# Two-layer hybrid decoder trunk: the second MLP product in pairs of half steps, its block sums on GpSimd, and the joint softmax issued earlier

## The chip, the cores and the metric

The kernel runs on one core of one Trainium2 chip. The metric is device time in microseconds (us) of one execution; the median of several is given, and one profiled execution is looked into. Engines: TensorE (PE), VectorE (DVE), ScalarE (ACT), GpSimd (POOL), and SyncE (SP), which issues most DMAs.

## What is computed

Two layers over 1024 tokens of width 1024, all in float32. The reference, cut to its core:

```python
for i in range(2):
    hn = rmsnorm(h, norm1[i])
    z = hn @ w_in[i]                       # u (256) | q, k, v (768 each)
    q, k = partial_rotary(q), partial_rotary(k)
    pool_out = pool_mixer(u, pool_w[i], pool_scale[i])   # windows 2, 4, 8, 16
    attn_out = dilated_mixer(q, k, v)      # 3 head groups, softmax over the groups' lse
    h = h + concat([pool_out, attn_out]) @ w_out[i]
    hn = rmsnorm(h, norm2[i])
    h = h + square(relu(hn @ w_up[i])) @ w_down[i]       # 1024 -> 4096 -> 1024
    gate = sigmoid(rmsnorm(h, norm3[i]) @ w_gate[i])
    h = h + gate * (p[i] @ w_ple[i])
return rmsnorm(h, final_norm)
```

In `dilated_mixer` three head groups (window 128, 512, 2048 at dilation 1, 4, 16) each give an output and a log-sum-exp; a softmax over the three log-sum-exps weighs the outputs.

## The kernel before, in words

Activations lie transposed, as tiles of 128 features by 1024 tokens. A float32 value is split into a high part (fp32r) and the rest, and a product is three matmuls (high x high, high x low, low x high) of 128x128 weights and 128x512 tokens. `split` makes the parts of an activation: ACT copies the high part, DVE subtracts (L500 to L506).

**One layer** on TensorE: the in-projection with the attention of three groups between (`attend`), the last value columns (`v2p`, L976 to L981), the out-projection (`po`), the up product (banks X, Y, Z with operand `xP`), the down product (banks X, Y, Z with operand `wP`), then gate and per-layer embedding (`gt`).

**Order.** One thread of Python issues everything. `Clock` holds a planned time: each matmul advances it (`tick`), generators (`ck.go`) issue other engines' operations and say with `yield ns` how long until their next one. `need` runs waiting generators until an operand has been issued. So the delays in nanoseconds set the order in which each engine gets its instructions; at run time the engines wait for each other by semaphores, and each engine keeps its order.

**Joint softmax** (`joint`, L897 to L928). After the 16 score statistics of each group, DVE takes the maximum over groups (L905, L906), subtracts (L908), ACT takes exp (L910), DVE sums and divides (L913 to L919), TensorE transposes the weights (`jt`, L922), DVE copies them out (`jw`, L925), a DMA writes them to DRAM (`wt_d`). `spread` reads them back, broadcast over 64 partitions (`wb`, from `W_0` on), `weigh` multiplies the head outputs (L950) and splits them for the out-projection.

**Both MLP products** use seven products in place of eight for blocks two by two (`Seven`, `products7`). `Seven.sums` forms four sums of weight blocks on POOL (L280 to L287), `make` splits each of the seven weight operands (ACT L299, DVE L301). A product `P1` to `P7` of a set goes to bank X, or to Y (`P2`) or Z (`P7`, `P4`); `Set.open` takes the bank, and `close` evacuates it after every product, because the next product into the same bank accumulates onto it. Tags: X has 3 banks ("mm"), Y and Z two each ("s", "e").

**Up product**: 16 sets of 256 features, each 7 products of 4 blocks x 3 matmuls. Its operands `xP` are made by `combine` and `xpiece` from the residual (L1007, L1009, L1071 to L1079). `Up.close` copies or adds banks into `y1` and `y2` (ACT L1131, DVE L1139 to L1146); `relu` takes relu times the norm factor on DVE (L1154) and the square on ACT (L1157); `sums` forms four block sums on DVE (L1172 to L1178) and writes seven pieces to DRAM (`x_d`).

**Down product**: `x_back` reads a piece from `x_d`, ACT copies its high part (L1192), DVE subtracts (L1194), giving `wP`. `STEPS` lists steps (t, a, b): output rows 2t and 2t+1, blocks a to b. There are 19 a layer: (3,0,3), (2,0,2), (1,0,1), then (a mod 4, a, min(a+4, 16)) for a = 0 to 15. The products of a step follow one another, and `Down.close` adds each into `acc` on DVE (L1210), 7 additions a step. After the last step of a row pair `rest` splits the result for the gate and feeds the third norm.

Small blocks of work such as 128x1024 tiles come from one pool of 49 blocks.

Of the kernel before, what the change touches and what calls it, by code (L numbers as in the profile page):

```python
# [9 lines left out]
F32 = mybir.dt.float32  # L10
# [27 lines left out]
T_M1, W_0, W_1 = 13000.0, 11000.0, 1800.0  # L38
# [3 lines left out]
STEPS = [(3, 0, 3), (2, 0, 2), (1, 0, 1)] + [(a % 4, a, min(a + 4, 16)) for a in range(16)]  # L42
# [72 lines left out]
def body(nc, tc, pools, A, out):  # L115
# [107 lines left out]
    class Seven:  # L223
# [10 lines left out]
        def __init__(self, sets, seq, name, lead=(12, 6, 4)):  # L234
# [3 lines left out]
            self.first = {}  # L238
            for q, (j, _) in enumerate(seq):
                self.first.setdefault(j, q)  # L240
            self.kicks = {}
            for j, q in self.first.items():
                self.kick(q - load, lambda j=j: self.load(j))
                self.kick(q - sums, lambda j=j: ck.go(self.sums(j)))
            for q, (j, P) in enumerate(seq):
                self.kick(q - make, lambda j=j, P=P: ck.go(self.make(j, P), (name, j, P)))

        def kick(self, q, fn):
            self.kicks.setdefault(q, []).append(fn)

        def lead(self, ns, step):

            for q in sorted(k for k in self.kicks if k < 0):
                for fn in self.kicks[q]:
                    ck.at(max(0.0, ns + q * step), fn)

        def at(self, q):
            for fn in self.kicks.get(q, ()):
                fn()

        def load(self, j):
            src, k0, n, c0 = self.sets[j]
            self.raw[j] = []
            for t in range(2):
                r = blk(f"{self.name}r{t}", F32, (128, n, 2, 128))
# [3 lines left out]
                self.raw[j].append(r)  # L269

# [3 lines left out]
        def sums(self, j):  # L274
            a11, a12, a21, a22 = (self.block(j, t, k) for t in range(2) for k in range(2))
            n = self.sets[j][2]
            s = [blk(f"{self.name}s0", F32, (128, 2, n, 128))]
# [6 lines left out]
            s.append(blk(f"{self.name}s1", F32, (128, 2, n, 128)))  # L284
# [23 lines left out]
    for L in range(DEPTH):  # L308
# [13 lines left out]
        for m in range(8):  # L322
            groups.append([(wo, 0, 8, 128 * m, 128, None)])
        sevens.append(([(wu, 0, 4, 256 * j) for j in range(FF // 256)],
                       [(wd, a, b - a, 256 * t) for t, a, b in STEPS]))
# [264 lines left out]
    def layer(L, hT, norm, tabs):  # L590
# [289 lines left out]

        for m in range(2):
# [13 lines left out]

        jd = small.tile([128, 3, 8, 4], F32, name="jd", tag="jd", bufs=1)

        def joint():
            while stats != [16, 16, 16]:
                yield 500.0  # L900
            yield 1500.0
            mx = small.tile([128, 8, 4], F32, name="jm", tag="jm", bufs=1)
            lf = small.tile([128, 3, 8, 4], F32, name="jl", tag="jl", bufs=1)
            dn = small.tile([128, 8, 4], F32, name="jn", tag="jn", bufs=1)
# [587 lines left out]
```

## Time and profile before

| | before |
|---|---|
| runs, us | 2370.68, 2370.72, 2378.85 |
| median, us | 2370.72 |
| profiled execution, us | 2371.51 |
| its span (first to last instruction), us | 2369.7 |
| mean granted TensorE clock | 0.987 |
| busy: TensorE / DVE / ACT / POOL | 97% / 72% / 43% / 30% |
| instructions in the span | 30964 |

How to read it: TensorE is the engine with the least idle time, so its pauses are what an order of work can change. The busy shares are means over stages; the views of waits, of single stretches and of time order below tell where TensorE pauses and what it waits for. "Granted clock" is the TensorE clock that was granted in a stretch, as a share of full speed. A wait is named as waiting line <- line that ended it.

### The profile page before, as it was taken

The page shows a single profiled execution, that of the slowest core. Times are in us where ns is not written, and L with a number is a line of the kernel's source. Part 1 is how long each engine was busy: PE and PEld are TensorE (multiplying, and loading weights), DVE is VectorE, ACT ScalarE, POOL GpSimd, SP SyncE. Part 2 cuts the span into 40 slices and gives each one's busy share as a digit, 9 for nine tenths or more (in the row PEclk, how much of TensorE's full clock was granted, in tenths as well). Part 3 has the DMA queues.
Part 4 walks back from the last instruction along what each step waited for, and adds up shares of the span by engine and source line. Part 5 has one row for each costly group of instructions (what it writes and reads, how often), then busy time and mean ns, then how long its engine had stood idle before and what let it go on. Part 6 is the DMA issues. An engine that isn't in the chain of part 4 may idle for free.

```text
span 2369.7 us, 30964 instructions
## 1 busy us (share of the span) xinstructions
PE 2299.1 (97%) x11088; PEld 1850.5 (78%) x11088; DVE 1711.4 (72%) x2888; ACT 1007.9 (43%) x2161; POOL 713.5 (30%) x562
## 2 busy tenths in 40 slices
PE   8999999999999999989999999999999989999898
PEld 6767778788887788877887767887888868888788
DVE  7555667787778888886565466677777798888845
ACT  5244533443335344444324344434433354443545
POOL 5111126323332433342221122253333233332422
PEclk9999999999999999999999999999999999999999
DMA  5011133255448555521120111333444485553214
GB/s 178 19 46 19 38 90 107 67 165 158 155 150 285 160 158 158 149 67 45 55 63 19 37 37 38 90 119 103 154 156 156 155 286 152 158 157 107 85 54 134
DMA packets 292401, 268.31 MB, mean 113 GB/s; under 512 B 12092, under 2 KB 223672, under 8 KB 292248
## 3 DMA queue, kind: packets, MB, share of 16 engines
q1 hardware_dynamic: 289656, 262.70, 36.5%
q0 software_dynamic: 2272, 3.61, 0.9%
q8 instruction: 87, 1.43, 0.2%
q14 instruction: 66, 0.54, 0.1%
q10 hardware_dynamic: 320, 0.03, 0.0%
HBM read 193.65 MB, written 72.58 MB: 112 GB/s over the span
## 4 chain that ended last, share of the span: by engine, by line
PE 46%; DVE 4%; ACT 1%; POOL 1%; DMA 1%; issue 1%; SPq 0%; DVEq 0%; ACTq 0%; POOLq 0%
PE X L535 13%; PE Z L535 7%; PE Y L535 3%; PE in L520 3%; PE in L518 3%; PE in L522 3%; PE gt L522 2%; PE gt L520 2%; PE gt L518 2%; PE s L752 1%; PE o L788 1%; DMA wP<-x_d 1%; PE e L774 1%; PE pl L520 1%; PE pl L522 1%
## 5 line engine op out<-in xcount | busy, mean ns | idle before, releaser
L535 PE MATMUL X<-wP,d1p 128*128 128x512 f32 x768 | 186.7, 393 | 15.0 <-DVE acc L1210 14.4
L535 PE MATMUL X<-wP,d0p 128*128 128x512 f32 x768 | 188.7, 396 | 12.8 <-DVE acc L1210 11.9
L535 PE MATMUL X<-xP,u0p 128*128 128x512 f32 x768 | 186.2, 394 | 3.9 <-ACT y L1131 3.9
L535 PE MATMUL X<-xP,u1p 128*128 128x512 f32 x768 | 185.8, 394 | 3.9 <-ACT y L1131 3.9
L1194 DVE TENSOR_TENSOR wP<-wP 128x512 fp32r<-128x512 f32 x224 | 183.4, 821 | 5.1 <-ACT wP L1192 5.1
L535 PEld LDWEIGHTS X<-wP,d1p 128*128 128x128 f32 x768 | 143.4, 188 | 51.0 <-ACT d1p L299 10.2
L535 PEld LDWEIGHTS X<-wP,d0p 128*128 128x128 f32 x768 | 144.6, 190 | 48.9 <-ACT d0p L299 9.1
L535 PEld LDWEIGHTS X<-xP,u0p 128*128 128x128 f32 x768 | 146.2, 191 | 35.3 <-ACT y L1131 4.7
L535 PEld LDWEIGHTS X<-xP,u1p 128*128 128x128 f32 x768 | 145.9, 190 | 35.2 <-ACT y L1131 4.8
L1157 ACT ACTIVATE y<-y 128x1024 f32<-128x1024 f32 x64 | 67.5, 1055 | 221.5 <-DVE y L1154 221.5
L1192 ACT ACTIVATE wP<-wP 128x512 fp32r<-128x512 f32 x224 | 137.9, 620 | 43.7 <-DMA wP<-x_d 43.3
L188 DVE SCALAR_TENSOR_TENSOR wl<-wr,gt,wh 128x128 fp32r<-128x128 f32 (+1 forms) x288 | 118.7, 443 | 38.5 <-ACT wh L194 38.2
L647 POOL TENSOR_TENSOR rot<-rot,s 128x512 f32<-128x512 f32 x48 | 61.5, 1284 | 277.2 <-DVE rot L645 216.2
L1210 DVE TENSOR_TENSOR acc<-acc,X 128x512 f32<-128x512 f32 x152 | 103.5, 682 | 33.7 <-PE X L535 29.9
L765 ACT ACTIVATE sm<-sm,nm 128x128 f32<-128x128 f32 (+1 forms) x192 | 84.5, 442 | 93.3 <-DVE nm L762 93.1
L194 ACT ACTIVATE wh<-wr,gt 128x128 fp32r<-128x128 f32 (+1 forms) x304 | 104.2, 396 | 0.8 <-DMA wr<-in_w_in_dram 0.7
L758 DVE CUSTOM_DVE_ANT_0 sm<-s,cst 128x128 f32<-128x128 f32 (+1 forms) x192 | 58.3, 346 | 52.0 <-PE s L752 52.0
L535 PE MATMUL Z<-xP,u1p 128*128 128x512 f32 x384 | 94.6, 394 | 0.3 <-DVE xP L1009 0.2
L535 PE MATMUL Z<-xP,u0p 128*128 128x512 f32 x384 | 94.4, 394 | 0.3 <-DVE xP L1009 0.2
L535 PE MATMUL Z<-wP,d0p 128*128 128x512 f32 x384 | 93.5, 390 | 0.0
L535 PE MATMUL Z<-wP,d1p 128*128 128x512 f32 x384 | 93.4, 389 | 0.0
L535 PEld LDWEIGHTS Z<-xP,u1p 128*128 128x128 f32 x384 | 72.9, 190 | 16.3 <-DVE xP L1009 0.5
(474 smaller groups left out, 5982.7 us busy)
## 6 DMA issues: line engine op xcount, KB each, us to landing
wP<-x_d SPq DMA_DIRECT2D x224, 256.0 KB, 2.8
x_d<-ys SPq DMA_DIRECT2D x64, 512.0 KB, 3.5
wr<-in_w_in_dram SPq DMA_DIRECT2D x40, 512.0 KB, 3.8
u0r<-in_w_up_dram SPq DMA_DIRECT2D x32, 512.0 KB, 5.3
x_d<-y SPq DMA_DIRECT2D x32, 512.0 KB, 2.8
u1r<-in_w_up_dram SPq DMA_DIRECT2D x32, 512.0 KB, 5.3
d0r<-in_w_down_dram SPq DMA_DIRECT2D x26, 512.0 KB, 5.2
d1r<-in_w_down_dram SPq DMA_DIRECT2D x26, 512.0 KB, 5.8
```

The source lines that it names most:

```text
L188: nc.vector.scalar_tensor_tensor(l[:, k], raw[:, k], gs[k], f(h[:, k]), op0=OP.mult, op1=OP.subtract)
L194: nc.scalar.activation(h[:, k], raw[:, k], AF.Copy, scale=gs[k])
L518: nc.tensor.matmul(p, wh, h[:, cols], start=first and i == 0, stop=False)
L520: nc.tensor.matmul(p, wh, l[:, cols], start=False, stop=False)
L522: nc.tensor.matmul(p, wl, h[:, cols], start=False, stop=last and i == n - 1)
L535: nc.tensor.matmul(p, w[:, a, i], x[:, b], start=first and i == 0 and a == b == 0, stop=i == n - 1 and a == 1, skip_group_check=not first)
L647: nc.gpsimd.tensor_tensor(a, a, tb["s"][:, hs(hf)], op=OP.mult)
L765: nc.scalar.activation(sm[:, i, hh], sm[:, i, hh], AF.Exp, bias=nm[:, j:j + 1], scale=0.125, accum_out=ml[g][:, n, 4 + h:5 + h])
L1157: nc.scalar.activation(y, y, AF.Square)
L1192: nc.scalar.activation(t[:, 0], f(t[:, 1]), AF.Copy)
L1194: nc.vector.tensor_tensor(t[:, 1], f(t[:, 1]), f(t[:, 0]), op=OP.subtract)
L1210: nc.vector.tensor_tensor(a, a, p, op=OP.add)
```

## The change

1. **Down product.** `STEPS` becomes 18 steps (t, a, n blocks): (2,0,2), (3,0,2), fourteen steps of 4 blocks in which output row pairs 0 and 1 take blocks 0 to 3, then 2 and 3 blocks 2 to 5, and so on by pairs, then (2,14,2), (3,14,2). The products of the first two steps alternate, and those of the last two. `Seven` plans its loads, sums and pieces in nanoseconds of product time (675 per block) in place of numbers of products, and steps of two blocks share a tile.
2. **Evacuation of the down product.** `P1` and `P6` (one addition each) are copied by ACT to a tile `out`, and POOL adds it to `acc`; the other five additions of a step stay on DVE.
3. **Block sums** of `y` go from DVE to POOL. The last two up sets alternate product by product.
4. **x_back** of sets 0 to 3 is issued with the last 14 products of the up product; inside the down product two sets are read back after each odd step.
5. **Joint softmax**: the generator starts before the u tiles are evacuated, and its delays (1500, 900, 400, 1200, 400 ns between its parts) become 900, 1800, 700, 3400, 500; `W_0` goes from 11000 to 6000; a wb tile is released when both halves used it.
6. **Up start**: in `combine` for the last row pair, 4500 in place of 900 before `P5`; the out-projection's last four banks are ("mm", "o", "e", "e") in place of ("s", "s", "e", "e"). `norm3.start` 7000 in place of 3000.

### The diff, cut to its core

```diff
-T_M1, W_0, W_1 = 13000.0, 11000.0, 1800.0
+T_M1, W_0, W_1 = 13000.0, 6000.0, 1800.0
...
-STEPS = [(3, 0, 3), (2, 0, 2), (1, 0, 1)] + [(a % 4, a, min(a + 4, 16)) for a in range(16)]
+ORDER = ("P1", "P7", "P6", "P2", "P5", "P4", "P3")
+STEPS = [(2, 0, 2), (3, 0, 2)] + [(2 * (i // 2 % 2) + i % 2, i // 2 * 2, 4) for i in range(14)]
+STEPS += [(2, 14, 2), (3, 14, 2)]
...
+                self.begin.append(t)
+                t += 675.0 * sets[j][2]
...
+        def kick(self, q, ahead, fn):
+            self.kicks.append((self.begin[q] - 2700.0 * ahead, fn))
...
+        def two(self, name, n, shape):
+
+            if n > 2:
+                return [lambda i=i: blk(f"{self.name}{name}{i}", F32, (128, *shape)) for i in range(2)]
+            b = []
+
+            def part(i):
+                if not b:
+                    b.append(blk(f"{self.name}{name}", F32, (128, 2, *shape)))
+                return b[0][:, i]
+            return [lambda i=i: part(i) for i in range(2)]
...
+        jd = small.tile([128, 3, 8, 4], F32, name="jd", tag="jd", bufs=1)
+
+        def joint():
+            while stats != [16, 16, 16]:
+                yield 500.0
+            yield 900.0
...
+        ck.go(joint(), "joint", 500.0)
+
         for m in range(2):
             def u_evac(p, hf, m=m):
...
-            if hf == 1:
+            used.append((g, p))
+            if used.count((g, p)) == 2:
                 del wbc[g, p]
...
-        ck.go(joint(), "joint", 500.0)
...
             ck.go(xpiece(i, "P6", T2))
-            yield 900.0
+            yield 900.0 if i < 3 else 4500.0
             ck.go(xpiece(i, "P5", T1))
...
-        seq = first + [(j, P) for j in range(2, n7) for P in ("P1", "P7", "P6", "P2", "P5", "P4", "P3")]
+        seq = first + [(j, P) for j in range(2, n7 - 2) for P in ORDER]
+        seq += [(j, P) for P in ORDER for j in (n7 - 2, n7 - 1)]
...
-        outs = [(bank(f"po{L}", ("s", "e")[k // 2]), wk(ws[k % 2], range(8)), hs(k // 2)) for k in range(4)]
+        outs = [(bank(f"po{L}", ("mm", "o", "e", "e")[k]), wk(ws[k % 2], range(8)), hs(k // 2)) for k in range(4)]
...
-                sub = nc.vector.tensor_tensor
+                sub = nc.gpsimd.tensor_tensor
...
                 sub(s[0][:, 0], b22, b12, op=OP.subtract)
+                yield 1400.0
...
-                    m = 2 * self.t + n
+                    m = 2 * STEPS[self.j][0] + n
                     a = acc[m][:, hs(hf)]
+                    if P in ("P1", "P6"):
+                        if P == "P1":
+                            self.out = blk("out")
+                        o = self.out[:, hs(n)]
+                        nc.scalar.activation(o, p, AF.Copy)
+                        ck.go(self.later(a, o))
+                        continue
                     nc.vector.tensor_tensor(a, a, p, op=OP.add)
...
+            def later(self, a, o):
+                yield 700.0
+                nc.gpsimd.tensor_tensor(a, a, o, op=OP.add)
...
-        seq2 = [(k, P) for k in range(len(STEPS)) for P in ORDER]
+        nst = len(STEPS)
+        seq2 = [(k, P) for P in ORDER for k in (0, 1)]
+        seq2 += [(k, P) for k in range(2, nst - 2) for P in ORDER]
+        seq2 += [(k, P) for P in ORDER for k in (nst - 2, nst - 1)]
...
-                D7.lead(7 * 12 * 225.0, 2700.0)
-                early = [(i, P) for P in ORDER for i in range(3)] + [(3, P) for P in ORDER]
-                for n, (i, P) in enumerate(early):
-                    ck.at(3200.0 + 1150.0 * n, lambda i=i, P=P: ck.go(x_back(i, P)))
+                D7.lead(8 * 12 * 225.0)
+            n = q - len(seq) + 15
+            if n > 0 and n % 2 == 0:
+                for i in range(4):
+                    ck.at((0.0, 1400.0, 15000.0, 17500.0)[i], lambda i=i, P=seq[q][1]: ck.go(x_back(i, P)))
...
-            run(D7, seq2, [q], live, lambda k: xw[STEPS[k][1]:STEPS[k][2]])
-            if k >= 3 and s.a + 4 < 16:
-                ck.go(x_back(s.a + 4, P))
+            run(D7, seq2, [q], live, lambda k: xw[a:a + n])
+            if n == 4 and t % 2 and a + 4 < 16:
+                ck.go(x_back(a + 4, P))
+                ck.at(9500.0, lambda i=a + 5, P=P: ck.go(x_back(i, P)))
...
-        norm3.start(3000.0)
+        norm3.start(7000.0)
```

### How it moves instructions

**TensorE at the joint softmax, layer 0** (`v2p` are products of the last value columns, `jt` the transpose of the joint weights, `o` an attention output). Before:

```order
1161 L976 MATMUL v2p_2897<-wh_2665,h_7H 128x256
1162 L977 MATMUL v2p_2897<-wh_2665,h_7L 128x256
1163 L978 MATMUL v2p_2897<-wl_2666,h_7H 128x256
1164 L922 MATMUL jt_2941<-cst,jt 96x128
1165 L976 MATMUL v2p_2943<-wh_2663,h_0H 128x256
1166 L977 MATMUL v2p_2943<-wh_2663,h_0L 128x256
```

With the change:

```order
1139 L998 MATMUL v2p_2908<-wh_2664,h_0H 128x256
1140 L999 MATMUL v2p_2908<-wh_2664,h_0L 128x256
1141 L1000 MATMUL v2p_2908<-wl_2665,h_0H 128x256
1142 L927 MATMUL jt_2912<-cst,jt 96x128
1143 L998 MATMUL v2p_2908<-wh_2664,h_1H 128x256
1144 L999 MATMUL v2p_2908<-wh_2664,h_1L 128x256
1145 L1000 MATMUL v2p_2908<-wl_2665,h_1H 128x256
1146 L808 MATMUL o_2917<-et_2559,v_0_2420 64x128 x4
```

`v2p_2897` before is `v2p_2908` now: the transpose stood behind all 24 products of this tile, and now behind its first three.

**ACT a little later in the same place** (L500, now L520, copies the high part of a weighted head; L981, now L1003, evacuates `v2p`; L800, now L820, evacuates `o`). Before:

```order
223 L800 ACTIVATE o_0_2422<-o_2989 128x128
224 L800 ACTIVATE o_0_2423<-o_2989 128x128
225 L981 ACTIVATE v_0_2420<-v2p_2979,r_a_429 128x256
226 L500 ACTIVATE cat_0H<-o_0_878 128x512 x2
227 L800 ACTIVATE o_0_2422<-o_3036 128x128
228 L800 ACTIVATE o_0_2423<-o_3036 128x128
```

With the change:

```order
223 L820 ACTIVATE o_0_2422<-o_2992 128x128
224 L820 ACTIVATE o_0_2423<-o_2992 128x128
225 L520 ACTIVATE cat_0H<-o_0_879 128x512
226 L520 ACTIVATE cat_0H<-o_0_878 128x512 x2
227 L1003 ACTIVATE v_0_2420<-v2p_2985,r_a_429 128x256
228 L520 ACTIVATE cat_0H<-o_0_879 128x512
```

Three copies of weighted heads, which depend on the joint weights, now stand ahead of the fourth evacuation of `v2p`; before they stood behind it.

**POOL at layer 0's down start** (`d0s` sums of weight blocks, `ys` block sums of y, `acc` additions to the down output). Before, the twelve operations that follow the last sums of up weights:

```order
179 L280 TENSOR_TENSOR d0s_6074<-d0r_6055,d0r_6057 128x384
180 L282 TENSOR_TENSOR d0s_6074<-d0r_6057 128x384
181 L285 TENSOR_TENSOR d0s_6115<-d0s_6074,d0r_6055 128x384
182 L287 TENSOR_TENSOR d0s_6115<-d0r_6055,d0s_6115 128x384
183 L280 TENSOR_TENSOR d0s_6267<-d0r_6182,d0r_6184 128x256
184 L282 TENSOR_TENSOR d0s_6267<-d0r_6184 128x256
185 L285 TENSOR_TENSOR d0s_6311<-d0s_6267,d0r_6182 128x256
186 L287 TENSOR_TENSOR d0s_6311<-d0r_6182,d0s_6311 128x256
187 L280 TENSOR_TENSOR d0s_6429<-d0r_6365,d0r_6367 128x128
188 L282 TENSOR_TENSOR d0s_6429<-d0r_6367 128x128
189 L285 TENSOR_TENSOR d0s_6464<-d0s_6429,d0r_6365 128x128
190 L287 TENSOR_TENSOR d0s_6464<-d0r_6365,d0s_6464 128x128
```

With the change, twelve operations from the last sums of the first two steps on:

```order
238 L307 TENSOR_TENSOR d0s<-d0r,d0s 128x256 x2
239 L1195 TENSOR_TENSOR ys_6280<-y_5986,y_5939 128x512
240 L1243 TENSOR_TENSOR acc_0_6265<-acc_0_6265,out 128x512
241 L1197 TENSOR_TENSOR ys_6280<-y_5939 128x512
242 L300 TENSOR_TENSOR d0s_6320<-d0r_6233,d0r_6235 128x512
243 L1243 TENSOR_TENSOR acc_0_6296<-acc_0_6296,out 128x512
244 L1195 TENSOR_TENSOR ys_6331<-y_6007,y_5962 128x512
245 L1199 TENSOR_TENSOR ys_6281<-y_5986,ys_6280 128x512
246 L302 TENSOR_TENSOR d0s_6320<-d0r_6235 128x512
247 L1197 TENSOR_TENSOR ys_6331<-y_5962 128x512
248 L1202 TENSOR_TENSOR ys_6281<-y_5986,ys_6281 128x512
249 L305 TENSOR_TENSOR d0s_6363<-d0s_6320,d0r_6233 128x512
```

The small sums of the steps of three, two and one block are gone; block sums of the last two up sets and additions to `acc` stand between the weight sums of the first full step.

## Rows read from the trace of the kernel before

**Rows 1.** The page of the profile: span, and busy time of each engine.

```profile
span 2369.7 us, 30964 instructions
...
PE 2299.1 (97%) x11088; PEld 1850.5 (78%) x11088; DVE 1711.4 (72%) x2888; ACT 1007.9 (43%) x2161; POOL 713.5 (30%) x562
```

**Rows 2.** TensorE's waits: line, awaited line, total us, times, longest us.

```profile
PE X L535 <- DVE acc L1210: 26.3, 19, 5.2
PE jt L922 <- DVE jt L919: 11.0, 2, 5.5
PE X L535 <- ACT y L1131: 7.8, 4, 3.1
```

**Rows 3.** TensorE by stretch: start:end, length, busy (matmuls), granted clock, DMA share, GB/s.

```profile
307.60:314.40 6.80, 5.82 (x29) 0.50 0.18 54
440.80:447.60 6.80, 6.13 (x15) 0.50 0.00 0
748.00:751.40 3.40, 3.40 (x10) 0.50 0.65 246
1058.60:1065.40 6.80, 4.61 (x10) 0.50 0.58 190
1471.60:1478.40 6.80, 5.04 (x26) 0.50 0.23 67
1604.70:1611.50 6.80, 5.66 (x13) 0.50 0.00 0
1906.00:1921.00 15.00, 9.83 (x43) 1.00 0.86 310
2225.90:2229.30 3.40, 3.13 (x7) 0.50 0.67 207
```

**Rows 4.** Steady down product: stretch, length, busy of PE, PEld, DVE, ACT, POOL, clock.

```profile
800.00:1000.00 200.00, 200.00 (x884) 165.60 (x883) 173.58 (x222) 85.31 (x148) 68.15 (x44) 1.00 0.52 149
```

**Rows 5.** Order of time at layer 0's joint softmax: start, us, engine, line, [idle before].

```profile
295.74 0.69 DVE L883 TENSOR_TENSOR u<-in,rs_a 128x512 f32<-128x512 f32 x1 [0.96 <-PE in L522]
...
297.01 2.70 DVE L178 TENSOR_TENSOR wl<-wr,wh 128x1024 fp32r<-128x1024 f32 x1
...
300.29 1.83 DVE L905 TENSOR_TENSOR jm<-mlp,mlp 128x32 f32<-128x32 f32 x1
...
296.52 2.11 POOL L830 TENSOR_TENSOR pa<-u 128x896 f32<-128x896 f32 x1 [28.00 <-DVE u L883]
...
300.24 1.83 POOL L830 TENSOR_TENSOR pb<-pa 128x768 f32<-128x768 f32 x1
...
308.58 0.45 PE L922 MATMUL jt<-cst,jt 128*96 128x128 f32 x1 [5.51 <-DVE jt L919]
```

**Rows 6.** Order of time, DVE, from the transposed weights to the first weighted head.

```profile
309.06 0.29 DVE L925 COPY jw<-jt 96x128 f32<-96x128 f32 x1 [0.54 <-PE jt L922]
316.78 1.29 DVE L950 TENSOR_TENSOR o<-o,wb 128x512 f32<-128x512 f32 x2 [7.43 <-DMA wb<-wt_d]
```

**Rows 7.** Order of time, ACT, at layer 0's up start.

```profile
438.25 1.15 ACT L1007 ACTIVATE xP<-t 128x512 fp32r<-128x512 f32 x2 [1.42 <-DVE t L1075]
440.30 0.63 ACT L1007 ACTIVATE xP<-t 128x512 fp32r<-128x512 f32 x1 [0.90 <-DVE t L1079]
440.83 1.07 ACT L1131 ACTIVATE y<-X 128x512 f32<-128x512 f32 x2
```

**Rows 8.** Order of time, TensorE, at the end of layer 0's down product.

```profile
1049.78 1.61 PE L535 MATMUL X<-wP,d0p 128*128 128x512 f32 x6 [0.85 <-DVE acc L1210]
...
1060.65 1.62 PE L535 MATMUL X<-wP,d0p 128*128 128x512 f32 x3 [5.19 <-DVE acc L1210]
```

**Rows 9.** Order of time, DVE, at layer 0's down start.

```profile
746.24 0.68 DVE L1194 TENSOR_TENSOR wP<-wP 128x512 fp32r<-128x512 f32 x1
746.84 0.67 DVE L1210 TENSOR_TENSOR acc<-acc,X 128x512 f32<-128x512 f32 x1
```

**Rows 10.** POOL's weight sums (L280), layer 0 up: ns min/median/max, first and last start.

```profile
L280 POOL TENSOR_TENSOR u0s<-u0r,u0r x16: 1288/1294/1737, 409.4 to 694.9; 128x512 f32<-128x512 f32 x16
```

More of the change, by code (lines that the diff above doesn't have):

```diff
@@ L276, in sums @@
             n = self.sets[j][2]
[L277 removed]
+            ss = self.two("s", n, (2, n, 128))
+            s = [ss[0]()]
             add = nc.gpsimd.tensor_tensor
@@ L879, in mixed @@
                 ck.waiting.discard((id(cat[m][0]), hf))
+        jd = small.tile([128, 3, 8, 4], F32, name="jd", tag="jd", bufs=1)
[3 more added lines that the diff above has]
+            yield 900.0
+            mx = small.tile([128, 8, 4], F32, name="jm", tag="jm", bufs=1)
+            lf = small.tile([128, 3, 8, 4], F32, name="jl", tag="jl", bufs=1)
+            dn = small.tile([128, 8, 4], F32, name="jn", tag="jn", bufs=1)
+            nc.vector.tensor_tensor(mx, mlp[0][:, :, 0:4], mlp[1][:, :, 0:4], op=OP.max)
+            nc.vector.tensor_tensor(mx, mx, mlp[2][:, :, 0:4], op=OP.max)
+            for g in range(3):
+                nc.vector.tensor_tensor(jd[:, g], mlp[g][:, :, 0:4], mx, op=OP.subtract)
+            yield 1800.0
+            nc.scalar.activation(jd, jd, AF.Exp, scale=0.125)
+            yield 700.0
+            for g in range(3):
+                nc.vector.tensor_tensor(lf[:, g], mlp[g][:, :, 4:8], jd[:, g], op=OP.mult)
+            nc.vector.tensor_tensor(dn, lf[:, 0], lf[:, 1], op=OP.add)
+            nc.vector.tensor_tensor(dn, dn, lf[:, 2], op=OP.add)
+            nc.vector.reciprocal(dn, dn)
+            jt = small.tile([128, 3, 4, 8], F32, name="jt", tag="jt", bufs=1)
+            for g in range(3):
+                nc.vector.tensor_tensor(jt[:, g].rearrange("p h t -> p t h"), jd[:, g], dn, op=OP.mult)
+            yield 3400.0
+            p = bank(f"jt{L}", "e")
+            nc.tensor.transpose(p[:96, :128], jt.rearrange("p g h t -> p (g h t)"), ident)
+            yield 500.0
+            w = small.tile([96, 128], F32, name="jw", tag="jw", bufs=1)
+            nc.vector.tensor_copy(w, p[:96, :128])
+            yield 300.0
+            nc.sync.dma_start(out=wt_d, in_=w)
+            yield 2200.0
+        ck.go(joint(), "joint", 500.0)
         for m in range(2):
@@ L893, in layer @@
         ck.go(mixed(1), delay=T_M1)
[L896 to L904, printed above, removed]
[L905 to L930 removed]
+        wbc, used = {}, []
         def spread(g, p):
```

91 lines of the change are left out of this document (31 added, 60 removed).

## The prediction, made before the changed kernel was run

> **What bounds the kernel now.** I read the table of engines first. TensorE is busy 2299.1 of 2369.7 us, 97% [rows 1]; the other engines are far below that. So some 70 us is all that a change of order can win, and work on VectorE (DVE), ScalarE (ACT) or GpSimd (POOL) costs only where TensorE waits for it. The number of matmuls stays: seven products, and the block counts of a layer's steps add up to 64 before (3+2+1, thirteen of 4, 3+2+1) and after (2+2, fourteen of 4, 2+2).
>
> Second, TensorE's waits, longest total first [rows 2]. Three lines are what the edits touch: 26.3 us for a product bank that DVE has still to add into `acc` (L1210), 11.0 us (twice 5.5) for the joint softmax, 7.8 us for a bank that ACT has still to copy at the start of the up product. Together 45.1 us.
>
> Third, the granted clock behind these waits [rows 3]. After four of layer 0's pauses TensorE runs at 0.50, the lower of its two levels (1.2 of 2.4 GHz): 6.8 us after the joint softmax, 6.8 at the up start, 3.4 at the down start, 6.8 at the down end; in layer 1 6.8, 6.8 and 3.4 at the joint, up start and down end. That is 5 times 6.8 and twice 3.4, 40.8 us, in which half the work was done, so 20.4 us are lost to it. It does not follow every pause: from 1906 to 1921, at the down start of layer 1, TensorE was busy only 9.83 of 15 us and the clock stayed at 1.00. The ceiling of the change is 45.1 + 20.4 = 65.5 us, over both layers.
>
> Fourth, a steady stretch of the down product [rows 4]: TensorE busy 200.00 of 200.00 us (884 matmuls, 0.226 us each), DVE 173.58, POOL 68.15. Nothing is to be won there, and something could be lost.
>
> **The measure.** The profiled execution took 2371.51 us, 1.8 more than its span and 0.8 more than the median of the three runs, 2370.72. Terms are taken from 2371.5, and 0.8 comes off at the end.
>
> **Joint softmax (two layers).** Before, DVE's chain stood behind a split of weights of 2.70 us (L178) and two more operations, and its first maximum took 1.83 us, because a POOL addition of 1.83 us had begun just before it [rows 5]. TensorE came to the transpose at 303.0 and began it at 308.58, after 5.51 us. Now the maxima and differences come ahead of the last `u` evacuation, in a gap of 0.96 us in which DVE waited for TensorE at 294.8; the rest still meets the POOL additions that this evacuation releases. Some seven two-input operations then pass between POOL operations of up to 2.11 us: I put the end at 302.3. TensorE comes 3.2 us earlier (25 matmuls), at 299.7, and waits 2.6. Saved 2.9 a layer. What is late next: ACT's queue. Three copies that need the weighted heads now stand ahead of the fourth evacuation of v. Before, the first weighting came 7.7 us after jw (309.06 to 316.78), 7.43 us of it a wait for the wb DMAs [rows 6]. jw now comes behind a weight split, at about 306, so the weighting at 313.7, the copies at 315 and v at 317; a TensorE at full clock would be there at 313.5. So the half clock that might be given back here is eaten by this wait. I take 2.5 a layer, 5. Ends: 0 (jw no earlier) and 11.0 + 6.8 = 17.8 (wait and clock both gone). The later wb loads of `W_0` and the counted release of wb move no other wait: 0, the copies are hidden as before.
>
> **Up start.** ACT made four xP copies before the two y copies that TensorE waited for: it began at 438.25, stood 0.90 us for DVE, and came to y at 440.83 [rows 7]. With 4500 instead of 900 the last two xP copies come after the y copies, so y can be copied 2.0 us earlier, at 438.8; xP5 and xP4 then come later and could be waited for themselves. The last out-projection banks lie elsewhere, so that the second product no longer waits for one of them; as it may wait for an xP instead, I cost that at 0. Taken: 2.0 a layer, 4. Ends: 0, and 7.8 + 6.8 (two windows at half clock) = 14.6.
>
> **Down start.** Of the 26.3 us, the ends of the down products have 0.85 + 5.19 a layer [rows 8], 12.1 in two; 14.2 are left for the starts. There the products of one step of 3, 2 or 1 blocks followed each other into one bank X, and DVE came to the addition late (746.84) because it had block sums and splits of 0.60 us each back to back [rows 9]. Now two steps of two blocks alternate, so that a bank rests for a product of 6 matmuls (1.4 us) between two of its own, the x pieces of sets 0 to 3 start up to 36 us ahead, the eight block sums of the last two sets and two additions of seven leave DVE. They go to POOL: 16 POOL operations of 128x512 fall in the 96 matmuls (21.7 us) after the first down product: 8 block sums, 4 sums of weights, 4 additions to `acc`. At 1.29 each [rows 10] that is 20.6 us. DVE has 26 operations with two SBUF inputs there; at 0.60, too much for the twelve of 256 columns, 15.6 us. If the two engines exclude each other, as at 300 us [rows 5], 36.2 us want into 21.7: 14.5 us over. Pieces of weights are made three steps of 2.7 us ahead in the planner, 8.1 us; that leaves 6.4. Between 0 and 6.4 I take 3.2 a layer, the middle, as the block sums of the last sets are not needed until the last steps. Saved 14.2 - 6.4 = 8. Ends: 14.2 + 1.7 (the window of 3.4 at half clock) gained, and with 14.5 a layer 29.0 - 14.2 = 14.8 lost.
>
> The Trainium skill speaks against this part. Its page "Perfetto Trace Analysis", section "Optimizing Scalar/DVE Operations", says that moving operations between GpSimd and DVE might not help, since they share an SBUF read port. The trace agrees as far as rows 5 go: a maximum of 32 columns took 1.83 us. By that rule this term would be its lower end, and the time the second rival's; the additions from PSUM (L1210) would keep their pace.
>
> **Down end.** TensorE stood 0.85 and 5.19 us and then ran 6.8 us at half clock [rows 8, 3]: products of 9, 6 and 3 matmuls were shorter than what DVE had to do for each. Now the last fourteen products have 6 matmuls and alternate between two steps, so twice the time passes between two evacuations of a bank, and two of seven go over ACT and POOL. Of 12.1 us of waits I take 10, and 3 of the 5.1 that the clock lost there (10.2 us at half): 13. Ends: 0 and 17.2. The later start of the third norm (7000) moves only its own eight small matmuls, which the gate's first products hide: 0.
>
> **Steady stretches.** Per two steps of four there is one stretch of 42 matmuls (9.5 us) with 5 POOL operations (6.5 us) and 9 two-input DVE operations (5.4 us): 11.9 us for the pair. The next stretches ask 6 to 8 us, and the pieces are made 8.1 us ahead, so I cost the 2.4 over at 0. Evacuations fall from 133 to 126 a layer; that was hidden.
>
> **Sum.** 5 + 4 + 8 + 13 = 30 us: 2341.5, less 0.8 is 2340.7, so 2341.
>
> **Rivals.**
> *Everything goes.* No wait is put in the place of the old ones and TensorE stays at 1.00: up to 65.5 us. With a fifth left standing, 53: 2318. For it: each named wait has an edit aimed at its cause. Against: the joint chain still meets POOL, and DVE was full at the down start.
> *POOL gives it back.* The pair of DVE and POOL costs the down start its low end, 14.8 lost, and the joint part gives nothing, while up start and down end give 17: 2371.5 - 2.2 - 0.8, or 2368, no change. For it: rows 5. Against: most of the moved sums are not urgent.
> *The pair binds in the whole down product.* It decides where the 2.4 us over of each heavy stretch cannot be carried into the light ones, because a small DVE operation waits out a whole POOL operation every time. Seven such stretches a layer: 14 times 2.4 is 33.6, with the down start's 14.8 on top, less 22 from the other parts: 2371.5 + 26.4 - 0.8, so 2397. For it: DVE is at 87% in the steady stretch [rows 4]. Against: L1210 reads PSUM and some DVE work goes away.
>
> **How the numbers follow.** Forecast 0.58 (its own range 2326 to 2356), everything goes 0.14, POOL gives it back 0.18, the pair binds 0.10. A measurement here tells 0.5% (11.9 us) from no change, so faster means under 2359: 0.58 + 0.14 and 0.02 of the second rival, 0.74; same 0.16; slower 0.10. The range takes in most of the first two rivals, 2314 to 2372, and leaves out the slow case, the upper part of the second rival and the best of the first, some 0.19.
>
> **What would show it.** Joint: a wait for jt of 2 to 4 us, and a new one of up to 3 us for an ACT evacuation of v. Up start: the first y copy ahead of 439.5. Down start: waits for `acc` of 2 to 5 us a layer, POOL busy almost throughout, DVE operations of 1.3 to 1.9 us between. Down end: no wait over 1.5 us. Steady down: TensorE without gaps. I am wrong if gaps show in the steady down product, or if TensorE waits for POOL's additions or sums.

## The result and the profile after

| | before | changed |
|---|---|---|
| runs, us | 2369.70 to 2378.85 (4) | 2393.32 to 2399.45 (4) |
| median, us | 2370.70 | 2396.45 |
| ratio, 95% interval | 1 | 1.0103 [1.0091, 1.0115] |
| profiled execution, us | 2371.51 | 2399.45 |
| its span, us | 2369.7 | 2397.7 |

The change makes the kernel slower, by 1.03%. I had forecast 2341, with 2314 to 2372 as range; the time lies beside the third rival's 2397. That this rival's sum was met is partly luck, as the steps below show. The experiments then part the loss, and one of them (e12), with the moved work kept, three times of issue altered and the up start put back, is faster than before.

The profiled execution of the changed kernel is the slowest of its four, with the lowest mean clock (0.981; the others have 0.982 to 0.985). So a few us of TensorE's busy time between two profiles don't prove anything about an edit.

The page of the changed kernel, span and busy time of each engine:

```profile
span 2397.7 us, 30878 instructions
...
PE 2308.6 (96%) x11088; PEld 1862.3 (78%) x11088; DVE 1621.3 (68%) x2660; ACT 1033.0 (43%) x2219; POOL 1016.5 (42%) x754
```

POOL has gone from 713.5 to 1016.5 us, DVE from 1711.4 to 1621.3 [rows 1]. The work was moved as read from the code. TensorE's waits now:

```profile
PE X L555 <- ACT out L1232: 20.9, 6, 6.7
PE Y L555 <- DVE wP L1218: 20.3, 12, 1.7
PE o L808 <- ACT v L1003: 6.1, 2, 3.2
...
PE ss_b L457 <- POOL sq_b L446: 4.6, 2, 2.3
PE X L555 <- DVE acc L1235: 3.0, 2, 2.0
PE jt L927 <- DVE cat_0L L526: 2.9, 1, 2.9
PE pp L1478 <- DVE p_1L L522: 2.8, 1, 2.8
PE jt L927 <- DVE cat_1L L526: 2.8, 1, 2.8
PE pp L1478 <- DVE p_0L L522: 2.6, 1, 2.6
PE X L555 <- ACT y L1154: 2.2, 2, 1.1
PE Z L555 <- ACT xP L1029: 2.1, 2, 1.1
```

Against [rows 2]: the 26.3 us for `acc` have become 20.9 for ACT's copy out (L1232) and 3.0 for `acc`, all at the two down starts; the down end's waits are gone. Twelve waits of 1.7 us for x pieces (`wP`) are new, as are those for the evacuation of v (L1003), and for the embedding's transposes (pp, L1478) at the gate. By place, in us over both layers (of before, a few lines too small for rows 2 are counted in: 1.2 for wP at the down start, 1.3, 0.6 and 0.4 at the up start, 3.5 for ss_c at the gate):

| place | before | forecast | after |
|---|---|---|---|
| joint softmax (jt, v) | 11.0 | 6 | 11.8 |
| up start (y, xP, res, ss_b) | 10.1 | 6 | 9.3 |
| down start | 15.4 | 6.4 | 23.9 |
| steady down product | 0 | 0 | 20.3 |
| down end | 12.1 | 2 | 0 |
| gate (ss_c, pp) | 3.5 | 3.5 | 5.4 |
| sum | 52.1 | | 70.7 |

So 18.6 of the 27.9 us between the two profiled executions are waits. The rest shows as busy time: TensorE is busy 2308.6 us after 2299.1 [rows 1], 9.5 more for the same 11088 matmuls. That is the lower clock at work. Stretches at 0.50 in the changed kernel, some of the fifteen before its tail, and their sum (stretch, length, TensorE busy, granted clock, DMA share, GB/s):

```profile
303.40:306.80 3.40, 3.40 (x20) 0.50 0.06 14
320.50:323.90 3.40, 3.40 (x18) 0.50 0.52 157
...
757.40:771.10 13.70, 8.45 (x19) 0.50 0.55 194
784.70:788.10 3.40, 3.34 (x8) 0.50 0.84 230
1091.90:1098.70 6.80, 6.80 (x26) 0.50 0.00 0
...
1935.00:1941.80 6.80, 2.92 (x6) 0.50 0.53 203
...
sum 85.10, PE 74.17; mean PE 4.95
```

Before there were eleven such stretches, the 40.8 us of [rows 3] and four more of 3.4, 54.4 together. Half of the 30.7 us more, 15.4, is the most that this can cost; it was less, because in some of them TensorE mostly stood (2.92 us busy of 6.80 at 1935).

The steady down product, which [rows 4] showed without a gap (stretch, length, busy of PE, PEld, DVE, ACT, POOL, clock, DMA share, GB/s):

```profile
800.00:1000.00 200.00, 191.53 (x841) 156.97 (x840) 156.24 (x190) 86.88 (x160) 94.07 (x60) 1.00 0.49 145
```

TensorE stands 8.5 of 200 us, though DVE has less to do than before (156.24 for 173.58). POOL has 94.07 for 68.15. One of these waits in order of time:

```profile
871.47 0.73 PE L555 MATMUL Y<-wP,d0p 128*128 128x512 f32 x2 [1.69 <-DVE wP L1218]
...
866.26 0.68 DVE L1235 TENSOR_TENSOR acc<-acc,Z 128x512 f32<-128x512 f32 x1
...
867.96 1.78 DVE L321 TENSOR_TENSOR d0p<-d0r,d0p 128x512 fp32r<-128x512 f32 x1
869.66 1.75 DVE L1218 TENSOR_TENSOR wP<-wP 128x512 fp32r<-128x512 f32 x1
...
865.86 1.63 POOL L305 TENSOR_TENSOR d0s<-d0s,d0r 128x512 f32<-128x512 f32 x1
867.57 1.63 POOL L307 TENSOR_TENSOR d0s<-d0r,d0s 128x512 f32<-128x512 f32 x1
869.15 1.72 POOL L1243 TENSOR_TENSOR acc<-acc,out 128x512 f32<-128x512 f32 x1
```

DVE's operations with two SBUF inputs take 1.75 us in place of 0.68 [rows 9] while a POOL operation of 1.6 to 1.7 us runs, and the addition from PSUM (L1235), which ran beside the POOL operation of 865.86, keeps its 0.68. The last x piece of a product ends in such a wait, at 871.4, and TensorE stands for it. The Trainium skill has this on the page "SBUF — State Buffer", section "Who interferes with whom": a VectorE instruction with two SBUF inputs contends with a GpSimd instruction that reads SBUF, and one with at most one SBUF input, outside VectorE's 2-port modes, does not. The trace agrees with both halves, 1.75 and 0.68.

At the down start of layer 0 the waits pass through several queues:

```profile
760.28 2.93 PE L555 MATMUL X<-wP,d0p 128*128 128x512 f32 x6 [5.55 <-ACT out L1232]
765.58 2.93 PE L555 MATMUL X<-wP,d0p 128*128 128x512 f32 x6 [2.38 <-ACT out L1232]
...
759.11 0.63 ACT L1216 ACTIVATE wP<-wP 128x512 fp32r<-128x512 f32 x1 [2.54 <-DMA wP<-x_d]
759.64 0.58 ACT L1232 ACTIVATE out<-X 128x512 f32<-128x512 f32 x1
764.63 0.42 ACT L319 ACTIVATE d0p<-d0r 128x256 fp32r<-128x256 f32 x1 [4.40 <-POOL ys L1197]
764.95 0.58 ACT L1232 ACTIVATE out<-X 128x512 f32<-128x512 f32 x1
...
754.09 0.69 DVE L1235 TENSOR_TENSOR acc<-acc,Z 128x512 f32<-128x512 f32 x1 [3.06 <-DMA acc<-h_d]
...
753.00 1.29 POOL L1243 TENSOR_TENSOR acc<-acc,out 128x512 f32<-128x512 f32 x1 [6.06 <-DMA acc<-h_d]
754.25 1.27 POOL L1197 TENSOR_TENSOR ys<-y 128x512 f32<-128x512 f32 x1
...
755.55 0.37 SPq L1200 DMA_DIRECT2D x_d<-ys  x1
756.02 0.43 SPq L1214 DMA_DIRECT2D wP<-x_d  x1
```

TensorE waits twice for a copy out. The second copy (764.95) stands in ACT's queue behind an operation that waits 4.40 us for a POOL block sum. The first and longer wait, 5.55 us, comes another way. Its copy (759.64) stands behind the copy of an x piece, which waited 2.54 us for its load. SyncE issued that load at 756.02, right behind a write of block sums (755.55), which had waited for POOL's sum of 754.25. And this sum stood behind an addition that waited 6.06 us for the DMA of `acc`.

At the joint softmax, TensorE, DVE and ACT in layer 0:

```profile
302.89 0.32 PE L927 MATMUL jt<-cst,jt 128*96 128x128 f32 x1 [2.85 <-DVE cat_0L L526]
319.14 0.66 PE L808 MATMUL o<-et,v 128*64 128x128 f32 x8 [3.16 <-ACT v L1003]
...
316.77 1.90 DVE L971 TENSOR_TENSOR o<-o,wb 128x512 f32<-128x512 f32 x3 [4.07 <-DMA wb<-wt_d]
...
317.50 1.23 ACT L520 ACTIVATE cat_0H<-o 128x512 fp32r<-128x512 f32 x2 [3.56 <-DVE o L971]
```

The transpose begins 5.7 us earlier than in [rows 5] and waits 2.85 instead of 5.51; sixteen us later TensorE gives 3.16 back, behind ACT's copies of weighted heads, which wait for DVE, which waits for the wb DMA.

### The profile page after: what moved, and what is told of

Its sections match the earlier page's. It is cut to its first block, busy times and chain, and to the rows that moved or that the text cites. A ratio compares the mean times of both kernels' runs of the same rounds, so it can differ in the third digit from the quotient of the medians.

```text
span 2397.7 us, 30878 instructions
## 1 busy us (share of the span) xinstructions
PE 2308.6 (96%) x11088; PEld 1862.3 (78%) x11088; DVE 1621.3 (68%) x2660; ACT 1033.0 (43%) x2219; POOL 1016.5 (42%) x754
## 4 chain that ended last, share of the span: by engine, by line
PE 78%; DVE 10%; issue 4%; ACT 3%; POOL 2%; DMA 2%; SPq 1%; DVEq 0%; ACTq 0%; POOLq 0%
PE X L555 26%; PE Z L555 13%; PE in L540 5%; PE in L538 5%; PE Y L555 5%; PE in L542 5%; PE gt L542 2%; PE gt L540 2%; PE gt L538 2%; DVE wP L1218 2%; PE s L772 2%; PE o L808 2%; PE e L794 1%; POOL res L1047 1%; DVE acc L1235 1%
## 5 line engine op out<-in xcount | busy, mean ns | idle before, releaser
L1218 DVE TENSOR_TENSOR wP<-wP 128x512 fp32r<-128x512 f32 x224 | 210.8, 949 | 6.9 <-ACT wP L1216 6.9
L555 PE MATMUL X<-wP,d0p 128*128 128x512 f32 x768 | 187.8, 397 | 11.6 <-ACT out L1232 10.4
L1243 POOL TENSOR_TENSOR acc<-acc,out 128x512 f32<-128x512 f32 x72 | 108.8, 1514 | 112.9 <-ACT out L1232 70.9
L1232 ACT ACTIVATE out<-X 128x512 f32<-128x512 f32 x72 | 42.8, 594 | 257.1 <-PE X L555 257.1
L1195 POOL TENSOR_TENSOR ys<-y,y 128x512 f32<-128x512 f32 x32 | 42.2, 1318 | 216.0 <-ACT y L1180 216.0
```

Of the source, the lines that this page charges most:

```text
L555: nc.tensor.matmul(p, w[:, a, i], x[:, b], start=first and i == 0 and a == b == 0, stop=i == n - 1 and a == 1, skip_group_check=not first)
L1218: nc.vector.tensor_tensor(t[:, 1], f(t[:, 1]), f(t[:, 0]), op=OP.subtract)
L1243: nc.gpsimd.tensor_tensor(a, a, o, op=OP.add)
```

## The experiments

Ratios are to runs of the kernel before on the same chip, with a 95% interval; times are medians.

**1. Block sums back on VectorE (e1).**

```diff
-                sub = nc.gpsimd.tensor_tensor
+                sub = nc.vector.tensor_tensor
```

> The changed kernel with one part undone: the four block sums of each up set are on VectorE again (with the old delays), everything else as changed. Changed kernel: TensorE stands 20.9 us for ACT's copy out (L1232, six times, all at the two down starts) and 20.3 us for the x pieces wP (twelve times 1.69 us, one in each heavy stretch of the steady down product). Theory A (GpSimd and VectorE exclude each other; the eight block sums at a down start keep GpSimd and so VectorE late): the waits at the down starts fall by half or more, 10 to 15 us, time 2381 to 2386; the twelve steady waits stay, because no block sum falls there. Theory B (the copies out stand in ACT's queue behind copies of x pieces that wait for their DMA): the waits at the down starts change by less than 4 us, time 2392 to 2400. Theory C (the pieces and acc simply arrive late by DMA): as B.

Measured: 2384.54 us, 1.0048 [1.0033, 1.0063]. The waits for the copy out fell from 20.9 to 8.5, those for `acc` rose from 3.0 to 5.1, and 0.9 for weight pieces came; the twelve steady waits stayed at 20.2. So 9.4 us of waits at the down starts hang on the block sums being on GpSimd, nearly the 10 that theory A asked for, and none of the steady ones do. The time moved by more, some 13 us; TensorE's busy time fell by 6.8 us too. B and C are excluded as whole explanations.

**2. Evacuations of P1 and P6 back on VectorE (e2).**

```diff
-                    if P in ("P1", "P6"):
-                        if P == "P1":
-                            self.out = blk("out")
-                        o = self.out[:, hs(n)]
-                        nc.scalar.activation(o, p, AF.Copy)
-                        ck.go(self.later(a, o))
-                        continue
```

> The changed kernel with the evacuations of P1 and P6 on VectorE again (no copy out on ACT, no addition on GpSimd); block sums stay on GpSimd. Theory A: the twelve waits of 1.69 us in the steady down product go (two of the five GpSimd operations of a heavy stretch are gone), 20 us; at the down starts some 5 us more: 2370 to 2376. Theory B: the 20.9 us for ACT's copy out go as well, and at most 5 us come back as waits for VectorE's addition: with the steady waits 2355 to 2362. Theory C: the steady waits may go, but the down starts keep their 20 us and more, now put down to VectorE's addition or the DMA of acc: 2374 to 2380. If the steady waits stay, their cause is when x_back is issued and not GpSimd: 2385 to 2396.

Measured: 2361.62 us, 0.9953 [0.9936, 0.9969]: this one part carries more than the whole loss. The steady waits fell from 20.3 to 6.0 (0.5 each), the waits before the gate from 5.4 to 0.4. At the down starts, though, 19.9 us stand for VectorE's addition in place of 20.9 for ACT's copy and 3.0 for `acc`. The time is in B's range, but not on B's way, which allowed 5 us there: as theory C had it, the waits at the down starts mostly changed their name. In the profile the gain is 19.4 us of TensorE's idle time, mostly the steady product and the gate, and 19.1 us of its busy time (clock 0.989 for 0.981).

**3. Both back on VectorE (e3).** The diffs of 1 and 2 together.

> The changed kernel with block sums and evacuations both on VectorE again: no work moved to GpSimd or ACT, only the order of steps, the earlier x pieces, the joint softmax and the up start remain changed. Theory A: all of the loss at the down product goes: 2352 to 2362 and faster than e2 by 5 to 12. Theory B: as e2 within 4. Theory C: the down starts still stand 15 to 20 us: 2372 or more.

Measured: 2359.91 us, 0.9945 [0.9930, 0.9960], not to be told from e2, as theory B had it. So once the evacuations are on VectorE, the block sums on GpSimd cost nothing that can be measured, against A's 5 to 12 (its range of 2352 to 2362 is met all the same). The down starts still stand 18.3 us for VectorE's addition, with none of the work moved; before the change they stood 14.2 for it. So the new order did not shorten them by itself.

**4. Weighted heads later (e4).**

```diff
-T_M1, W_0, W_1 = 13000.0, 6000.0, 1800.0
+T_M1, W_0, W_1 = 13000.0, 11000.0, 1800.0
```

> The changed kernel with W_0 at 11000 again: the weighted heads are issued later, so that ACT's three copies stand behind the fourth evacuation of v, as before. TensorE stood 6.1 us for that evacuation (twice 3.05) and 5.7 for the joint transpose (twice 2.85). Theory D (ACT's queue turned the joint gain into a new wait): the 6.1 us go, time 4 to 9 us below the changed kernel, 2387 to 2392. Rival: the wait moves on to the next thing that needs the weights (the out-projection's first operand), time within 2 us of the changed kernel.

Measured: 2386.23 us, 1.0056 [1.0041, 1.0071], 0.47% under the changed kernel's ratio, some 11 us. The waits for v are gone from the list and jt keeps its 2.9 and 2.8. Theory D holds. The gain is above the 6.1 us of waits, and more than its 9 at most: TensorE's busy time fell by 8.6 us as well (mean granted clock from 0.981 to 0.985). How much of that belongs to these waits is not shown.

**5. The first acc loads earlier, with all sums on VectorE (e5).** To e3:

```diff
+            if q == len(seq) - 6:
+                for m in range(4, 8):
+                    acc[m] = blk(f"acc{m}_{L}")
+                    nc.sync.dma_start(out=acc[m], in_=h_d[m])
```

> As e3 (block sums and all evacuations on VectorE), and the four loads of acc tiles that the first two steps need are issued six products (16.6 us) before the down product, not at its first product. In e3 VectorE stood 3.78 us for acc<-h_d at the first addition, whose load was issued at 741.8 and landed near 748.7, and TensorE stood 8.8 and 9.5 us in the two down starts. Theory C (what the alternating pairs wait for at the down start are data that arrive late, the four acc loads at once first of all): the waits there fall by at least 4 us a layer, time 2346 to 2353. Rival (VectorE is full there, or the x pieces of sets 2 and 3 are late anyway): the first wait goes and the next ones grow, time within 4 us of e3, 2356 to 2363; the loads then only delay the x pieces, in whose front they are now issued.

Measured: 2359.52 us, 0.9950 [0.9935, 0.9965], the same as e3. The waits for `acc` went from 19.3 to 16.7 us, the longest from 3.1 to 6.4, and 1.5 us for the copy of an x piece came. The first wait went and a later one grew: the rival holds for this kernel.

**6. Only GpSimd's additions to VectorE, ACT's copies stay (e6).**

```diff
-                nc.gpsimd.tensor_tensor(a, a, o, op=OP.add)
+                nc.vector.tensor_tensor(a, a, o, op=OP.add)
```

> The changed kernel with only the additions of the copied banks moved from GpSimd to VectorE: ACT still copies P1 and P6 out, and VectorE adds the copy to acc. It parts the two halves of the evacuation. Theory A (GpSimd's additions make VectorE wait): the twelve waits of 1.69 us in the steady down product go or fall to 0.5, as in e2, and the 5.4 us before the gate (pp for p) go; time 2366 to 2380. Theory B (ACT's queue): 15 us or more are still named as waits for ACT's copy out at the down starts, as ACT still stands for the DMAs of x pieces in front of it. If the steady waits stay at 1.69 us, the copies on ACT and not GpSimd are their cause: 2390 or more.

Measured: 2362.89 us, 0.9963 [0.9951, 0.9974]. The stretch in the steady down product:

```profile
800.00:1000.00 200.00, 198.09 (x865) 161.32 (x864) 163.33 (x218) 89.33 (x167) 60.37 (x40) 1.00 0.50 150
```

TensorE is busy 198.09 us in place of 191.53; of the twelve steady waits six are left, 2.8 us together. The waits before the gate fell from 5.4 to 2.6. No wait for the copy out is left in the list, though the copies stand in ACT's queue as before. The time is lower than theory A's 2366, the mechanism is A's. Theory B falls: ACT's queue, with its DMAs, is not enough. In the steady product it was GpSimd's additions that made the evacuation dear. At the down starts taking them away gave less: in place of 20.9 for the copy out and 3.0 for `acc` stand 6.3 for `acc` and 11.6 for weight pieces.

**7. The old up start and the later weights, on e3 (e7).** W_0 as in 4, and

```diff
-            yield 900.0 if i < 3 else 4500.0
+            yield 900.0
...
-        outs = [(bank(f"po{L}", ("mm", "o", "e", "e")[k]), wk(ws[k % 2], range(8)), hs(k // 2)) for k in range(4)]
+        outs = [(bank(f"po{L}", ("s", "e")[k // 2]), wk(ws[k % 2], range(8)), hs(k // 2)) for k in range(4)]
```

> As e3, with W_0 at 11000 and the up start undone as well (900 in place of 4500 before P5, the last out-projection banks s, s, e, e). In e3 the up starts stood 6.5 and 6.0 us (before: 4.3 and 4.4), of which 4.1 a layer for ss_b, that is for GpSimd's sums of squares, and 1.7 for the evacuation of v. Theory E (the reordered up start only moved its wait to ss_b): the ss_b waits fall to under 1 us, the wait for ACT's y copy of 3.1 comes back, and with W_0 the v wait goes: 0 to 6 us faster than e3, 2354 to 2360. Rival (the new up start is worth its 2 us a layer): 2 to 5 us slower than e3, 2361 to 2365.

Measured: 2356.00 us, 0.9934 [0.9917, 0.9950]; the interval overlaps e3's. ss_b went from 7.7 to 2.0, v from 1.7 to nothing, y from 3.7 back to 7.8. The new up start moved its wait; whether it is worth an us or costs one is not told by these runs, as `W_0` was moved with it.

**8. e5 and e7 together (e8).**

> e5 and e7 together: block sums and evacuations on VectorE, acc loads early, W_0 at 11000, the old up start. If both steps hold they add up: 2341 to 2349, the fastest so far. If only one holds, 2350 to 2357.

Measured: 2353.21 us, 0.9927 [0.9912, 0.9942]: the time is that of one step holding. The interval overlaps those of e5 and e7, so the runs do not tell which.

**9. The changed kernel with the first acc loads earlier (e9).** The diff of 5, on the changed kernel.

> The changed kernel (block sums and additions on GpSimd) with the four first acc loads issued six products earlier, as in e5. In the changed kernel GpSimd stood 6.06 us for acc<-h_d at its first addition, with block sums and weight sums behind it in its queue, and ACT stood 4.40 us for a block sum before it came to the copy out that TensorE waited for. Theory F (GpSimd's queue is held at its head by the addition that waits for acc, and everything behind it with it): without that wait the 20.9 us for ACT's copy out fall by half or more, the twelve steady waits of 1.69 us stay; time 2380 to 2388. Rival (GpSimd's work itself is too much there, whoever holds its head): the waits at the down starts change by less than 4 us, time 2392 to 2400.

Measured: 2386.20 us, 1.0058 [1.0043, 1.0073]. Its waits:

```profile
PE Y L555 <- DVE wP L1218: 20.3, 12, 1.7
PE X L555 <- ACT out L1232: 11.7, 2, 5.8
```

The same edit that gave nothing in e5 is worth 0.45%, some 11 us, here. There VectorE waited for the load and nothing but its own work was behind; here GpSimd did, and block sums and weight sums behind it. The time is in theory F's range. Its mechanism holds for 9.2 of the 20.9 us, a little less than the half that it asked for: of six waits two are left, and 3.3 us more stand for `acc` and 1.7 for weight pieces. In the profile TensorE's idle time fell by only 3.3 us and its busy time by 11.5, so much of the gain is the clock.

**10. The second x pieces earlier, on e8 (e10).**

```diff
-                ck.at(9500.0, lambda i=a + 5, P=P: ck.go(x_back(i, P)))
+                ck.at(7000.0, lambda i=a + 5, P=P: ck.go(x_back(i, P)))
```

> As e8, with the second x_back of each odd step 7.0 instead of 9.5 us after the first. e8 still stands twelve times some 0.48 us for wP (5.8 us). Theory G (those pieces are only issued too late by the plan): the 5.8 us fall below 2 us, time 2347 to 2350 against 2353.2. Rival (VectorE is full there): the waits stay or move, time 2351 to 2356.

Measured: 2351.48 us, 0.9913 [0.9897, 0.9930], the lowest of all, within the interval of e8. The waits for wP went from the list, and waits of 0.33 us for `acc` took their place: the rival's case, waits that move.

**11. The same edit on the changed kernel (e11).**

> The changed kernel with the second x_back of each odd step 7.0 instead of 9.5 us after the first, nothing else. Theory A (VectorE waits out GpSimd's operations there): the twelve waits of 1.69 us get smaller by what the pieces start earlier only in part, as the sums and additions of GpSimd still fall on them: 8 us or more stay, time 2384 to 2392. Theory G (the plan issues them too late, GpSimd only takes the slack): they vanish, 20 us less: 2374 to 2380.

Measured: 2369.68 us (10 runs), 0.9987 [0.9977, 0.9996]. One number takes back the whole loss, some 27 us, more than theory G's 20. In the profile 17.8 us of it are TensorE's idle time and 11.9 its busy time, the mean clock having gone from 0.981 to 0.985; why the clock is higher was not tried. The steady stretch:

```profile
800.00:1000.00 200.00, 200.00 (x884) 165.46 (x883) 166.74 (x198) 93.15 (x172) 100.99 (x65) 1.00 0.52 156
```

and the groups of x pieces on VectorE, of the changed kernel and then of this one (count, busy, mean ns, idle before):

```profile
L1218 DVE TENSOR_TENSOR wP<-wP 128x512 fp32r<-128x512 f32 x224 | 210.8, 949 | 6.9 <-ACT wP L1216 6.9
```

```profile
L1218 DVE TENSOR_TENSOR wP<-wP 128x512 fp32r<-128x512 f32 x224 | 217.6, 979 | 6.6 <-ACT wP L1216 6.6
```

TensorE has no gap, while GpSimd is as busy (100.99 us) and VectorE's operations are no faster: 979 ns in the mean, after 949, and 821 before. So theory G holds, and A as the reason of the slowness but not of the loss: the pieces came late by the plan, and GpSimd took the slack that would have hidden most of it. Without the additions on GpSimd (e2, e3) TensorE still waited 0.5 us for an x piece, twelve times.

**12. Everything retimed, the work left on GpSimd (e12).** The changed kernel with the diffs of 4, 5, 7 and 10.

> e10 with the block sums and the evacuations of P1 and P6 moved to ACT and GpSimd again, as the change has them: the changed kernel with acc loads six products earlier, the second x_back at 7.0 us, W_0 at 11000 and the old up start. It tells whether the moved work itself costs time once the transfers come early. Theory H (the loss came from pieces and acc arriving late, and the moved work only took the slack that hid it): within 5 us of e10, 2347 to 2357. Rival (the moved work keeps a price of its own: the copies out behind ACT's queue at the down start, 11.7 us in e9, and 5.4 us before the gate): 2360 to 2370.

Measured: 2354.82 us, 0.9930 [0.9913, 0.9946]; e10's 0.9913 lies at its lower end. The two times are 3.3 us apart, within the 5 of theory H, which holds; whether the moved work costs these 3.3 us is not told by these runs. With the same work on GpSimd and ACT as in the change, three times of issue (`W_0`, the `acc` loads, the second x piece) and the old up start turn 1.0103 into 0.9930. The two waits that the rival priced are there, 11.6 and 5.4 us. But e10 stands 16.8 us for `acc` at its own down starts, and between 800 and 1000 us TensorE is busy 200.00 us in e12 and 198.37 in e10. What is left against e10 in its waits:

```profile
PE X L555 <- ACT out L1232: 11.6, 2, 5.8
PE X L555 <- DVE acc L1235: 6.9, 4, 3.2
...
PE pp L1482 <- DVE p_1L L522: 2.8, 1, 2.8
```

The 5.8 us still come through GpSimd: ACT stood 6.51 us for a block sum before the copy out. Its operation there copies weights and doesn't compute with that sum; I suppose it takes over the sum's buffer, and have not tried it.

```profile
755.34 0.42 ACT L319 ACTIVATE d0p<-d0r 128x256 fp32r<-128x256 f32 x1 [6.51 <-POOL ys L1202]
755.66 0.58 ACT L1232 ACTIVATE out<-X 128x512 f32<-128x512 f32 x1
```

## Why the prediction was wrong

**Steady stretches: the step that failed first.** I wrote that the pieces are made 8.1 us ahead, and so costed the 2.4 us over in each heavy stretch at 0. The 8.1 us are the lead of weight pieces. An x piece has its own plan, and the second of each pair is issued 9.5 us after the first; there was too little lead to draw on. Measured: twelve waits of 1.69 us, 20.3 us. The third rival had priced fourteen at 2.4, 33.6, with the right place and the right pair of engines; but its condition, that the pair cannot do the work in time, is refuted by e11, where the same work leaves TensorE busy 200.00 of 200.00 us. So that the time met its 2397 is in part luck: its losses of 33.6 and 14.8 were 20.3 and 8.5, its gains of 22 were 10.2 over all other places, and the 9.5 us of busy time that were not in its sum made up for it.

**Down start: saved 8 was forecast, 8.5 was lost.** The forecast let the new order clear all 14.2 us and the moved work take 6.4 back. The first of these failed by itself: with nothing moved (e3) the down starts stood 18.3 us for `acc`, and with the loads early as well (e5) 15.7; which of the work queued on VectorE keeps them there is open. For the moved work I priced GpSimd's sixteen operations by their durations and let the planner's lead hide part. What I left out is the order in its queue: the first addition to `acc` waited 6.06 us for a load, and block and weight sums stood behind it; issuing that load earlier (e9) took 9.2 us off the waits for the copy out. I also took it that block sums of the last sets are not needed until the last steps. Their values are not, but ACT's queue (4.40 us) and SyncE's waited for them, and behind those stood the copies out for which TensorE waited. This is the loss of the rival "POOL gives it back" (14.8), smaller and by another way.

**Joint softmax: 5 forecast, nothing came.** The wait for jt was foreseen at 2.6 and measured 2.85. The new wait for v was named, with its place in ACT's queue, up to 3 us; it was 3.16. The mistake was in setting this wait against the clock alone, and not against the gain itself. I also costed the moved loads of wb (`W_0`) at 0. In the trace of layer 0 the first of them is issued earlier, at 307.06 us instead of 311.97, and with `W_0` back at 11000 (e4) the wait for v goes and the kernel gains some 11 us. What the earlier start of the joint chain is worth by itself was not tried.

**Up start: 4 forecast, 0.8 in waits.** y's wait fell from 7.8 to 2.2, by more than the 4 forecast, but waits for xP (2.1) and, unforeseen, for GpSimd's sums of squares (ss_b, 4.6) took the room.

**Down end: 13 forecast; right for the waits.** 12.1 us of waits are 0, in the changed kernel and in all variants but for waits under 0.8 us. This is what the fast variants keep. The other 3 us were to come from the clock. The stretch at 0.50 left the down end, but one of 6.80 us stands a little later, at the gate (1091.90). Over the whole kernel TensorE's busy time rose by 9.5 us, where the sum had only these 3 us, as a gain.

**The gate.** I costed the later norm at 0. The 3.5 us for ss_c went, but 5.4 for the embedding's transposes came; they fall to 0.4 in e2 and e3 and to 2.6 in e6. So they hang on the moved evacuation, about half of them on GpSimd's additions alone. The later norm was not undone by itself.

By the rule of the Trainium skill that moving work between GpSimd and VectorE might not help ("Perfetto Trace Analysis", "Optimizing Scalar/DVE Operations"), I gave a chance of 0.28 to the rivals that followed from it. The trace bears it out for the change as it stands: against e3, which has the same order and nothing moved, GpSimd has 308.6 us more (1016.5 for 707.9) and VectorE only 49.5 less (1621.3 for 1670.8). The runs add that the times of issue decide what this costs: e12 has the same moves, is 0.7% faster than before, and within 0.2% of e10, which has none.

## What to carry to other kernels

Price a moved operation by its queue: what stands in front of it, what it may wait for there, and who stands behind; here an addition that waited 6.06 us for a DMA held up block sums, and through two more queues TensorE. When a slower engine takes work, look for the operand with the least lead, for each operand's own plan, before concluding that an engine is too slow: one delay of 9.5 us made 7.0 gave back some 27 us. Test the parts of a change by undoing them one at a time, as its losses (here 20.3 us in the steady product and 8.5 at the down starts) can hide a gain (here 12.1 us at the down end).

## What the runs showed of the hardware that was not expected

VectorE's slow operations are not a loss by themselves: with a mean of 979 ns for 821 before, TensorE had no gap in 200 us. An operation of 32 columns can take as long as one of 512: 1.83 us at the joint softmax before [rows 5], 1.75 us for a full one in the changed kernel. The lower clock level followed pauses in stretches of 3.4, 6.8 and, at the down start of the changed kernel, 13.7 us (757.40 to 771.10). In that one TensorE was busy 8.45 us between and after waits of 5.55 and 2.38 us, and the clock did not rise between them.
